# Score matmuls over all 128 rows with a zero-filled second half, and norm factors spread by PE transposes of a broadcast column

## The chip, the core and the metric

The program runs on one core of a Trainium2 chip. The core has five engines that run their own instruction streams and meet through semaphores: PE (TensorE: matrix products, with a separate stream of weight loads, PEld), DVE (VectorE), ACT (ScalarE), POOL (GpSimd) and SP (which issues most DMAs). A matmul multiplies a stationary operand, loaded first, with a moving operand that streams through, and writes to PSUM. The metric is the device time of one execution in microseconds, as the median of several runs. Smaller is better.

## What is computed

Three transformer-like blocks run one after the other on one sequence of 1024 tokens of width 1024, in 32-bit floats. Block 1 mixes differential attention (4 heads, each with two score maps of head size 64) with chunked retention, then a feed-forward layer. Block 2 mixes neighbourhood attention, a convolution, pooling and a gating unit. Block 3 mixes a sliding-window attention (8 query heads of size 64 in 4 groups, a window of 128 tokens), a gated recurrent layer computed in chunks, a cross-attention and a feed-forward layer with a convolution. RMS norms stand between all of them. The parts that the change touches are these:

```python
def rms_norm(x, g, eps=NORM_EPS):
    xf = x.astype(jnp.float32)
    y = xf * lax.rsqrt(jnp.mean(xf * xf, axis=-1, keepdims=True) + eps)
    return (y * g.astype(jnp.float32)).astype(x.dtype)
...
        scores = jnp.einsum('bhmqd,bhmkd->bhmqk', qblk, kt) + bias[None, :, None]
        p = jax.nn.softmax(scores, axis=-1)
        a = p[:, :, 0] - lam * p[:, :, 1]
...
    s = jnp.einsum('bnqhgd,bnkhd->bnhgqk', qb, kw).astype(jnp.float32) * (D ** -0.5)
```

## The kernel before

Features lie on the 128 partitions and tokens on the free axis, in two halves of 512 tokens (`h` is 0 or 1). To keep 32-bit accuracy with the one-pass matmul type, every operand is split into a high and a low part (`split`, L143 on ACT for the high part, L145 on DVE or POOL for the low part), and a product is three matmuls, high by high, high by low and low by high (`mm3`, L178 to L180). `dense` is one output tile of 128 features by 512 tokens: eight such triples, 24 matmuls.

**The scores.** A head has 64 features, so one score map needs 64 rows of the array. The kernel stacks: `qs[m]` holds for map `m` the high part of q on 64 partitions and its low part on the other 64, and `ks[m]` holds the high part of k on both halves (the copies are made by DMA). One matmul over 128 rows (L539, in the window attention L1459) then gives high by high plus low by high. The missing term, q high by k low, is a second matmul into the same PSUM tile over 64 rows alone (L540, L1460), with `kl`, one tile in which map 0 uses partitions 0 to 63 and map 1 partitions 64 to 127. In block 1 `attn_diff` makes these pairs per head, query block, map and stretch of up to 512 keys. DVE then takes the pair's result out of PSUM with bias and row maximum (L544). In block 3 `window` makes them per group, block of 128 queries and map, over 256 keys (128 at the start of the sequence).

**The norm factors.** `rstd` sums squares over features with matmuls against a column of ones (`mean_col`, L204), gets the factor with a power on POOL (`rsqrt_col`, L217, tile `rr`: one column for each 128 tokens, token on the partition), and must then lay it out along the free axis, the same on all partitions (`spread`). `spread` splits the factor into `rh` and `rl` (L225, L227 on DVE), builds two diagonal matrices by multiplying the identity (L231, twice 128x512 on DVE) and adds two matmuls of a matrix of ones with them (L237). DVE reads the result as an operand when it scales (L272, L510, L1268 and others).

**The order of the work.** The kernel is written with generators that interleave streams, and a scheduler places the instructions of each engine by a simulated timeline and a priority; each engine then runs its list strictly in order. Long-lived tiles come from a pool of 37 slots of equal size (`SLOTS`, `slot`); who asks for a slot when none is free waits until all readers of some slot have ended. While a head of `attn_diff` runs, `proj_ret` of the same head and, once slots are free, `proj_diff` of the next supply other matmuls to put between the scores. PSUM tiles of the kind `s` (scores) have three banks in both stages, those of kind `d` (`dense`) two.

Of the kernel before, what the change touches and what calls it, by code (L numbers as in the profile page):

```python
# [18 lines left out]
P = 128  # L19
T = 1024  # L20
# [38 lines left out]
class Env:  # L59
# [160 lines left out]
    def spread(self, r):  # L220

        nc = self.nc
        n = r.shape[-1]
        rh = self.small.tile([P, n], F32R, tag="rh", name="rh")
        nc.vector.tensor_copy(rh, r)  # L225
        rl = self.small.tile([P, n], F32R, tag="rl", name="rl")
        nc.vector.tensor_tensor(rl, r, rh.bitcast(F32), op=ALU.subtract)  # L227
        out = self.pt()[:, : n * P]
        for i, q in enumerate((rh, rl)):
            dg = self.tmp.tile([P, n, P], F32R, tag="diag", bufs=2, name="diag")  # L230
            nc.vector.tensor_tensor(  # L231
                dg,
                self.ident[:, None, :].broadcast_to([P, n, P]),
                q.bitcast(F32)[:, :, None].broadcast_to([P, n, P]),
                op=ALU.mult,
            )
            nc.tensor.matmul(out, lhsT=self.ones_r, rhs=dg.rearrange("p a b -> p (a b)"), start=i == 0, stop=i == 1)  # L237
        return out
# [121 lines left out]
def block1(e, next_gain):  # L360
# [45 lines left out]
    with ExitStack() as c2:  # L406
# [38 lines left out]
        def proj_diff(hd):  # L445

            scale = 0.125 * 2.0 ** (2 * (hd + 1))
            ts = [e.slot("qk", (T,), F32R) for _ in range(5)]
            qs, ks, kl = ts[0:2], ts[2:4], ts[4]
            wq = e.chunk(io["w1_fm"][hd])  # L450
            wk = e.chunk(io["w1_fm"][4 + hd])
            for h in range(2):
                sl = half(h)
                ql = e.tsq(dt=F32R)
                p = normed(e.dense(wq, hs[h]), h)
                for m in range(2):
                    b = slice(64 * m, 64 * m + 64)
                    nc.scalar.activation(qs[m][b, sl], p[b], AF.Copy, scale=scale)
                    nc.vector.scalar_tensor_tensor(ql[b], p[b], scale, qs[m][b, sl].bitcast(F32), op0=ALU.mult, op1=ALU.subtract)
                p = normed(e.dense(wk, hs[h]), h)  # L460
                for m in range(2):
                    b = slice(64 * m, 64 * m + 64)
                    nc.scalar.activation(ks[m][b, sl], p[b], AF.Copy)
                    nc.vector.tensor_tensor(kl[b, sl], p[b], ks[m][b, sl].bitcast(F32), op=ALU.subtract)
                for m in range(2):
                    b = slice(64 * m, 64 * m + 64)
                    o = slice(64 - 64 * m, 128 - 64 * m)
                    nc.sync.dma_start(qs[m][o, sl].bitcast(F32), ql[b].bitcast(F32))
                    nc.sync.dma_start(ks[m][o, sl].bitcast(F32), ks[m][b, sl].bitcast(F32))
# [48 lines left out]
        def attn_diff(hd, ops, v):  # L518
# [3 lines left out]
            for pr in range(4):  # L522
# [6 lines left out]
                for i in range(2):  # L529
# [3 lines left out]
                    for m in range(2):  # L533
                        mx = None
                        pc = []
                        for c, n in cols:
                            s = e.pss()[:, :n]
                            b = slice(64 * m, 64 * m + 64)
                            nc.tensor.matmul(s, lhsT=qs[m][:, blk(qb)], rhs=ks[m][:, c : c + n], start=True, stop=False)  # L539
                            nc.tensor.matmul(s, lhsT=qs[m][b, blk(qb)], rhs=kl[b, c : c + n], start=False, stop=True)  # L540
# [780 lines left out]
def block3(e, acc, hs, rest, out):  # L1321
# [39 lines left out]
    with ExitStack() as c2:  # L1361
# [10 lines left out]
        def stack(w, scale, h, qs, kl=None):  # L1372

            p = e.dense(w, hs[h])
            ql = e.tsq(dt=F32R) if kl is None else kl
            for m in range(2):
# [3 lines left out]
                nc.vector.scalar_tensor_tensor(ql[b], p[b], scale, qs[m][b].bitcast(F32), op0=ALU.mult, op1=ALU.subtract)  # L1380
                nc.sync.dma_start(qs[m][o].bitcast(F32), (ql[b] if kl is None else qs[m][b]).bitcast(F32))
# [36 lines left out]
        kl = e.slot("kl", (T,), F32R)  # L1418
        va = e.slot("va", (8, P))

        def window_kv(h):
            stack(e.chunk(io["w3_fm"][4]), 1.0, h, [k[:, half(h)] for k in ks], kl[:, half(h)])
# [21 lines left out]
        def window(g, h):  # L1444
            qs = ops[g, h][4]
            po = e.po()
            for j4 in range(4):
# [9 lines left out]
                for m in range(2):  # L1457
                    b = slice(64 * m, 64 * m + 64)
                    nc.tensor.matmul(s[m], lhsT=qs[:, m, blk(j4)], rhs=ks[m][:, k0 : k0 + wd], start=True, stop=False)  # L1459
                    nc.tensor.matmul(s[m], lhsT=qs[b, m, blk(j4)], rhs=kl[b, k0 : k0 + wd], start=False, stop=True)  # L1460
# [358 lines left out]
```

## Time and profile before

| | |
|---|---|
| median of 3 runs | 3494.2 us (3491.73 to 3495.17) |
| the profiled execution | 3490.75 us, of which the profile's span is 3489.0 us |
| PE busy | 3329.4 us (95% of the span), 16510 matmuls |
| DVE, ACT, POOL busy | 1922.8 us (55%), 1348.9 us (39%), 894.9 us (26%) |
| mean granted TensorE clock | 0.974 of full speed |

The time of one execution is its span and 1.75 us around it. The profile was taken in an execution that ran 3.45 us under the median of the three runs. A matmul's row gives its start and a modelled duration that overlaps the next matmul; what a matmul costs on PE is read from one start to the next, not from the duration.

### The profile page before, as it was taken

To read this page: it belongs to the slowest core of one execution; us is meant where nothing else is said; L and a number is where in the kernel's file an instruction comes from. 1 tells how busy PE (TensorE), PEld (TensorE's weight loads), DVE (VectorE), ACT (ScalarE), POOL (GpSimd) and SP (SyncE) were. 2 spreads that over 40 slices of the span, in tenths; PEclk is the share of its full clock that TensorE was granted. 3 is DMA by queue.
4 is the path that set the end of the run, shared out by engine and by line. 5 is a ranking of instruction groups with operands and counts; after the bars stand their busy time and mean duration, and the time that the engine had idled before them with its cause. 6 is when DMAs were issued, how large, how long until landed. Compare 5 with 4: busy or idle time off the path is not lost.

```text
span 3489.0 us, 43291 instructions
## 1 busy us (share of the span) xinstructions
PE 3329.4 (95%) x16510; PEld 2737.6 (78%) x16510; DVE 1922.8 (55%) x3463; ACT 1348.9 (39%) x2354; POOL 894.9 (26%) x577
## 2 busy tenths in 40 slices
PE   7999998999999999889999899999899999999997
PEld 6788877888888887677667778878887788888886
DVE  8566566622222238984777575776635771434346
ACT  4444453412211233333544455554443442313132
POOL 2000013401100113521334444435333430202021
PEclk8999999999999999999999999999999999999999
DMA  4112123211111114345644221224423321111114
GB/s 126 46 44 59 49 77 125 94 58 43 46 53 53 43 60 139 115 120 164 204 153 133 74 68 58 82 85 151 151 67 103 133 93 57 47 53 44 53 42 146
DMA packets 122431, 306.23 MB, mean 88 GB/s; under 512 B 17008, under 2 KB 25584, under 8 KB 122224
## 3 DMA queue, kind: packets, MB, share of 16 engines
q1 hardware_dynamic: 122224, 303.47, 27.1%
q8 instruction: 130, 2.13, 0.3%
q14 instruction: 77, 0.63, 0.1%
HBM read 256.23 MB, written 40.37 MB: 85 GB/s over the span
## 4 chain that ended last, share of the span: by engine, by line
PE 38%; DVE 6%; issue 3%; ACT 2%; POOL 1%; DMA 0%; DVEq 0%; POOLq 0%; ACTq 0%
PE ps_d L178 11%; PE ps_d L180 11%; PE ps_d L179 11%; PE ps_s L1548 1%; ACT whi L143 1%; DVE act L145 1%; DVE ssum L263 0%; POOL wlo L145 0%; PE ps_o L1482 0%; PE ps_t L204 0%; DVE hSA L1549 0%; DVE pr L1124 0%; PE ps_s L1460 0%; DVE nq L272 0%; PE ps_d L1559 0%
## 5 line engine op out<-in xcount | busy, mean ns | idle before, releaser
L180 PE MATMUL ps_d<-act,wlo 128*128 128x512 f32 x2272 | 894.2, 394 | 14.5 <-DVE wlo L145 13.2
L178 PE MATMUL ps_d<-act,whi 128*128 128x512 f32 x2272 | 895.6, 395 | 8.0 <-ACT whi L143 4.3
L179 PE MATMUL ps_d<-act,whi 128*128 128x512 f32 x2272 | 895.9, 394 | 3.0 <-DVE act L145 3.0
L143 ACT ACTIVATE whi<-raw 128x1024 fp32r<-128x1024 f32 (+2 forms) x394 | 387.4, 984 | 969.9 <-PE ps_d L179 854.3
L145 POOL TENSOR_TENSOR wlo<-raw,whi 128x1024 fp32r<-128x1024 f32 (+1 forms) x162 | 391.9, 2422 | 740.1 <-ACT whi L143 714.2
L180 PEld LDWEIGHTS ps_d<-act,wlo 128*128 128x128 f32 x2272 | 429.8, 189 | 109.6 <-DVE wlo L145 17.1
L178 PEld LDWEIGHTS ps_d<-act,whi 128*128 128x128 f32 x2272 | 430.0, 189 | 103.3 <-ACT whi L143 9.2
L179 PEld LDWEIGHTS ps_d<-act,whi 128*128 128x128 f32 x2272 | 429.9, 189 | 98.9 <-issue 6.5
L145 DVE TENSOR_TENSOR wlo<-raw,whi 128x1024 fp32r<-128x1024 f32 (+2 forms) x232 | 259.1, 1117 | 276.5 <-ACT whi L143 276.0
L180 PE MATMUL ps_d<-up,wlo 128*128 128x512 f32 x864 | 336.5, 389 | 0.0
L179 PE MATMUL ps_d<-up,whi 128*128 128x512 f32 x864 | 336.2, 389 | 0.0
L178 PE MATMUL ps_d<-up,whi 128*128 128x512 f32 x864 | 335.5, 389 | 0.0
L686 POOL TENSOR_TENSOR nt<-sq 128x512 f32<-128x512 f32 x64 | 83.5, 1305 | 556.0 <-ACT sq L684 555.1
L180 PE MATMUL ps_d<-mix,wlo 128*128 128x512 f32 x512 | 202.6, 396 | 2.9 <-POOL wlo L145 2.9
L178 PE MATMUL ps_d<-mix,whi 128*128 128x512 f32 x512 | 201.1, 399 | 3.3 <-DVE acc L643 2.1
L179 PE MATMUL ps_d<-mix,whi 128*128 128x512 f32 x512 | 203.0, 397 | 0.0
L180 PEld LDWEIGHTS ps_d<-up,wlo 128*128 128x128 f32 x864 | 162.2, 188 | 34.0 <-DVE wlo L145 0.3
L179 PEld LDWEIGHTS ps_d<-up,whi 128*128 128x128 f32 x864 | 162.2, 188 | 33.8
L178 PEld LDWEIGHTS ps_d<-up,whi 128*128 128x128 f32 x864 | 162.2, 188 | 33.7
L693 DVE TENSOR_TENSOR acc<-ps_d,acc 128x512 f32<-128x512 f32 x96 | 66.4, 692 | 203.9 <-PE ps_d L180 203.9
L217 POOL TENSOR_TENSOR rr<-rv,mhalf 128x4 f32<-128x4 f32 (+1 forms) x43 | 45.8, 1065 | 486.3 <-DVE rv L211 274.6
L178 PE MATMUL ps_d<-whi,act 128*128 128x256 f32 x512 | 151.8, 299 | 19.4 <-ACT act L388 12.6
(404 smaller groups left out, 5528.5 us busy)
## 6 DMA issues: line engine op xcount, KB each, us to landing
raw<-in_w_up SPq DMA_DIRECT2D x94, 512.0 KB, 3.3
raw<-in_w_fm SPq DMA_DIRECT2D x84, 512.0 KB, 3.6
raw<-in_w_out SPq DMA_DIRECT2D x42, 512.0 KB, 3.3
raw<-in_w_down SPq DMA_DIRECT2D x64, 320.0 KB, 3.0
xd<-acc SPq DMA_DIRECT2D x64, 256.0 KB, 2.4
acc<-xd SPq DMA_DIRECT2D x64, 256.0 KB, 5.5
raw<-in_w_down SPq DMA_DIRECT2D x32, 384.0 KB, 3.2
raw<-in_w_tm SPq DMA_DIRECT2D x22, 512.0 KB, 3.3
```

What stands on the lines that cost most here:

```text
L143: nc.scalar.activation(hi, src, AF.Copy)
L145: e.tensor_tensor(lo, src, hi.bitcast(F32), op=ALU.subtract)
L178: nc.tensor.matmul(out, lhsT=wh, rhs=xh, start=start, stop=False)
L179: nc.tensor.matmul(out, lhsT=wh, rhs=xl, start=False, stop=False)
L180: nc.tensor.matmul(out, lhsT=wl, rhs=xh, start=False, stop=stop)
L217: self.nc.gpsimd.tensor_tensor(r, v, self.mhalf.broadcast_to([P, n]), op=ALU.pow)
L686: nc.gpsimd.tensor_tensor(u, r, r, op=ALU.mult)
L693: nc.vector.tensor_tensor(acc[f][:, h], p, acc[f][:, h], op=ALU.add)
L1548: nc.tensor.matmul(s[:, blk(j, 64)], lhsT=x[:, blk(j)], rhs=xv[:, nb * j : nb * j + nb, 1], start=True, stop=True)
```

## The change

The change has two parts.

*Scores.* `kl` becomes two tiles, one for each map, both 128 partitions high. The 64 partitions that the map does not use are set to zero once by POOL (two memsets of 64x1024 for each head in `proj_diff`, two in the window attention). The second score matmul then runs over all 128 rows, with the same stationary operand as the first. Each of the two attentions holds one slot more: six instead of five for a head's q and k, and one more for the whole window stage.

*Norm factors.* `spread` no longer splits the factor or builds diagonals. For each of the (usually four) columns it transposes that column, read 128 times with a step of zero, on PE against the identity. The 128x128 result has the factor of token t in column t on all partitions.

```diff
     def spread(self, r):
-        rh = self.small.tile([P, n], F32R, tag="rh", name="rh")
-        nc.vector.tensor_copy(rh, r)
-        rl = self.small.tile([P, n], F32R, tag="rl", name="rl")
-        nc.vector.tensor_tensor(rl, r, rh.bitcast(F32), op=ALU.subtract)
         out = self.pt()[:, : n * P]
-        for i, q in enumerate((rh, rl)):
-            dg = self.tmp.tile([P, n, P], F32R, tag="diag", bufs=2, name="diag")
-            nc.vector.tensor_tensor(dg, self.ident[:, None, :]..., q..., op=ALU.mult)
-            nc.tensor.matmul(out, lhsT=self.ones_r, rhs=dg..., start=i == 0, stop=i == 1)
+        for i in range(n):
+            nc.tensor.transpose(out[:, blk(i)], r[:, i : i + 1].broadcast_to([P, P]), self.ident)
         return out
...
         def proj_diff(hd):
-            ts = [e.slot("qk", (T,), F32R) for _ in range(5)]
-            qs, ks, kl = ts[0:2], ts[2:4], ts[4]
+            ts = [e.slot("qk", (T,), F32R) for _ in range(6)]
+            qs, ks, kl = ts[0:2], ts[2:4], ts[4:6]
+            for m in range(2):
+                nc.gpsimd.memset(kl[m][64 - 64 * m : 128 - 64 * m].bitcast(F32), 0.0)
...
-                            nc.tensor.matmul(s, lhsT=qs[m][b, blk(qb)], rhs=kl[b, c : c + n], start=False, stop=True)
+                            nc.tensor.matmul(s, lhsT=qs[m][:, blk(qb)], rhs=kl[m][:, c : c + n], start=False, stop=True)
...
-        kl = e.slot("kl", (T,), F32R)
+        kl = [e.slot(f"kl{m}", (T,), F32R) for m in range(2)]
+        for m in range(2):
+            nc.gpsimd.memset(kl[m][64 - 64 * m : 128 - 64 * m].bitcast(F32), 0.0)
...
-                    nc.tensor.matmul(s[m], lhsT=qs[b, m, blk(j4)], rhs=kl[b, k0 : k0 + wd], start=False, stop=True)
+                    nc.tensor.matmul(s[m], lhsT=qs[:, m, blk(j4)], rhs=kl[m][:, k0 : k0 + wd], start=False, stop=True)
```

The scheduler places everything anew, so instructions shift by a few places all over the program. Three places show what moves. The first is PE in the first head of `attn_diff`, where single score pairs stand between projection matmuls (`ps_s` is a score tile, `ps_d` a projection, `ps_t` a transpose). Before:

```order
L178 MATMUL ps_d<-act,whi 128x512
L539 MATMUL ps_s<-qk 128x512
L540 MATMUL ps_s<-qk 128x512
L179 MATMUL ps_d<-act,whi 128x512
L180 MATMUL ps_d<-act,wlo 128x512
L178 MATMUL ps_d<-act,whi 128x512
```

After, the same place:

```order
L178 MATMUL ps_d<-act,whi 128x512
L558 MATMUL ps_t<-ident,prob 128x128
L529 MATMUL ps_s<-qk 128x512
L530 MATMUL ps_s<-qk 128x512
L179 MATMUL ps_d<-act,whi 128x512
L180 MATMUL ps_d<-act,wlo 128x512
```

A transpose has moved in front of the pair, and the pair itself stands as it stood; the lines 529 and 530 are the old 539 and 540. The second place is DVE at the end of the program, from the last mean to the last scaling. Before:

```order
L207 TENSOR_SCALAR rv<-ps_t 128x4
L225 CAST rh<-rr 128x4
L227 TENSOR_TENSOR rl<-rr,rh 128x4
L231 TENSOR_TENSOR diag<-ident,rh 128x512
L231 TENSOR_TENSOR diag<-ident,rl 128x512
L1268 SCALAR_TENSOR_TENSOR acc<-acc,g_ffn_post_norm_14656,ps_t 128x512 x8
```

After, DVE has two rows there, and PE's list ends with the four mean columns and four transposes of the factor:

```order
L207 TENSOR_SCALAR rv<-ps_t 128x4
L1258 SCALAR_TENSOR_TENSOR acc<-acc,g_ffn_post_norm_14512,ps_t 128x512 x8
```

```order
L204 MATMUL ps_t<-ones_r,ssum 128x1 x4
L226 MATMUL ps_t<-ident,rr 128x128 x4
```

The four DVE instructions between mean and scaling are gone. The third place is POOL at the change from head 0 to head 1 of block 1 (`rr` is a norm factor, `nt` a gated output of the retention). Before:

```order
L217 TENSOR_TENSOR rr<-rv,mhalf 128x4 x3
L512 TENSOR_TENSOR nt<-nt,gate 128x512
L217 TENSOR_TENSOR rr<-rv,mhalf 128x4
L512 TENSOR_TENSOR nt<-nt,gate 128x512
L217 TENSOR_TENSOR rr<-rv,mhalf 128x4 x3
```

After, the same place:

```order
L217 TENSOR_TENSOR rr<-rv,mhalf 128x4
L440 MEMSET qk 64x1024 x2
L217 TENSOR_TENSOR rr<-rv,mhalf 128x4 x2
L503 TENSOR_TENSOR nt<-nt,gate 128x512
L217 TENSOR_TENSOR rr<-rv,mhalf 128x4
L503 TENSOR_TENSOR nt<-nt,gate 128x512
```

The two memsets of the next head stand between the two factors of the differential attention, so a factor of the same head waits behind them.

## Rows read from the trace of the kernel before

**Rows 1.** The profile page: span, and each engine's busy time (share, xinstructions).
```profile
span 3489.0 us, 43291 instructions
...
PE 3329.4 (95%) x16510; PEld 2737.6 (78%) x16510; DVE 1922.8 (55%) x3463; ACT 1348.9 (39%) x2354; POOL 894.9 (26%) x577
```

**Rows 2.** Busy time by stretch: PE, PEld, DVE, ACT, POOL, granted clock, DMA share, GB/s.
```profile
110.00:480.00 370.00, 369.34 (x2041) 302.65 (x2040) 216.96 (x550) 164.56 (x361) 20.92 (x18) 1.00 0.17 51
1950.00:2350.00 400.00, 377.56 (x2200) 313.21 (x2200) 270.50 (x634) 225.47 (x443) 180.15 (x154) 0.94 0.22 71
```

**Rows 3.** PE's groups, shapes apart: rows*columns, xcount, busy, mean ns, idle before.
```profile
L540 PE MATMUL ps_s<-qk 64*128 64x512 f32 x64 | 32.4, 506 | 0.0
...
L1460 PE MATMUL ps_s<-kl,swq 64*128 64x256 f32 x56 | 22.5, 402 | 0.0
...
L540 PE MATMUL ps_s<-qk 64*128 64x256 f32 x32 | 12.8, 400 | 0.0
...
L1460 PE MATMUL ps_s<-kl,swq 64*128 64x128 f32 x8 | 2.6, 323 | 0.0
```

**Rows 4.** Timeline of PE in block 1's attention: start, duration, instruction.
```profile
88.85 0.39 PE L178 MATMUL ps_d<-act,whi 128*128 128x512 f32 x1
89.08 0.40 PE L539 MATMUL ps_s<-qk 128*128 128x512 f32 x1
89.40 0.50 PE L540 MATMUL ps_s<-qk 64*128 64x512 f32 x1
89.83 0.50 PE L179 MATMUL ps_d<-act,whi 128*128 128x512 f32 x1
90.17 0.40 PE L180 MATMUL ps_d<-act,wlo 128*128 128x512 f32 x1
```

**Rows 5.** Timeline of the weight loads at the same place.
```profile
89.40 0.18 PEld L540 LDWEIGHTS ps_s<-qk 64*128 64x128 f32 x1 [0.36 <-issue]
...
90.17 0.19 PEld L178 LDWEIGHTS ps_d<-act,whi 128*128 128x128 f32 x1
```

**Rows 6.** Timeline of PE in block 3's window attention, a pair over 256 keys.
```profile
2172.24 0.28 PE L1459 MATMUL ps_s<-k,swq 128*128 128x256 f32 x1
2172.44 0.38 PE L1460 MATMUL ps_s<-kl,swq 64*128 64x256 f32 x1
2172.75 0.50 PE L179 MATMUL ps_d<-act,whi 128*128 128x512 f32 x1
2173.09 0.39 PE L180 MATMUL ps_d<-act,wlo 128*128 128x512 f32 x1
```

**Rows 7.** Timeline of PE, two full-height matmuls of 256 columns in a row.
```profile
2188.52 0.28 PE L179 MATMUL ps_d<-wlo,act 128*128 128x256 f32 x1
2188.64 0.28 PE L180 MATMUL ps_d<-whi,act 128*128 128x256 f32 x1
```

**Rows 8.** Timeline of PE around three transposes.
```profile
91.33 0.49 PE L568 MATMUL ps_t<-ident,prob 128*128 128x128 f32 x3
...
91.89 0.39 PE L180 MATMUL ps_d<-act,wlo 128*128 128x512 f32 x1
```

**Rows 9.** Timeline at the program's last norm, all engines.
```profile
3472.84 1.02 POOL L217 TENSOR_TENSOR rr<-rv,mhalf 128x4 f32<-128x4 f32 x1 [9.59 <-DVE rv L207]
...
3474.92 1.40 PE L237 MATMUL ps_t<-diag,ones_r 128*128 128x512 f32 x2 [2.35 <-DVE diag L231]
...
3476.35 4.04 DVE L1268 SCALAR_TENSOR_TENSOR acc<-acc,g_ffn_post_norm,ps_t 128x512 f32<-128x512 f32 x6 [0.89 <-PE ps_t L237]
```

**Rows 10.** What PE waited for: us in total, times, longest.
```profile
PE ps_t L237 <- DVE diag L231: 14.1, 7, 3.0
...
PE ps_s L539 <- ACT act L143: 4.3, 1, 4.3
```

**Rows 11.** DVE's group of the first of the two diagonals.
```profile
L231 DVE TENSOR_TENSOR diag<-ident,rh 128x512 fp32r<-128x512 f32 x46 | 31.5, 685 | 7.1 <-PE ps_t L237 7.1
```

**Rows 12.** POOL's group of the memset that is nearest in size.
```profile
L875 POOL MEMSET cb<- 128x1024 f32 x2 | 1.9, 952 | 0.0
```

More of the change, by code (lines that the diff above doesn't have):

```diff
@@ L223, in spread @@
         n = r.shape[-1]
-        rh = self.small.tile([P, n], F32R, tag="rh", name="rh")
-        nc.vector.tensor_copy(rh, r)
-        rl = self.small.tile([P, n], F32R, tag="rl", name="rl")
-        nc.vector.tensor_tensor(rl, r, rh.bitcast(F32), op=ALU.subtract)
         out = self.pt()[:, : n * P]
-        for i, q in enumerate((rh, rl)):
-            dg = self.tmp.tile([P, n, P], F32R, tag="diag", bufs=2, name="diag")
[L231 to L237, printed above, removed]
+        for i in range(n):
+            nc.tensor.transpose(out[:, blk(i)], r[:, i : i + 1].broadcast_to([P, P]), self.ident)
         return out
@@ L463, in proj_diff @@
                     nc.scalar.activation(ks[m][b, sl], p[b], AF.Copy)
-                    nc.vector.tensor_tensor(kl[b, sl], p[b], ks[m][b, sl].bitcast(F32), op=ALU.subtract)
+                    nc.vector.tensor_tensor(kl[m][b, sl], p[b], ks[m][b, sl].bitcast(F32), op=ALU.subtract)
                 for m in range(2):
@@ L1374, in stack @@
             p = e.dense(w, hs[h])
-            ql = e.tsq(dt=F32R) if kl is None else kl
+            if kl is None:
+                ql = e.tsq(dt=F32R)
             for m in range(2):
@@ L1379, in stack @@
                 nc.scalar.activation(qs[m][b], p[b], AF.Copy, scale=scale)
-                nc.vector.scalar_tensor_tensor(ql[b], p[b], scale, qs[m][b].bitcast(F32), op0=ALU.mult, op1=ALU.subtract)
-                nc.sync.dma_start(qs[m][o].bitcast(F32), (ql[b] if kl is None else qs[m][b]).bitcast(F32))
+                lo = ql[b] if kl is None else kl[m][b]
+                nc.vector.scalar_tensor_tensor(lo, p[b], scale, qs[m][b].bitcast(F32), op0=ALU.mult, op1=ALU.subtract)
+                nc.sync.dma_start(qs[m][o].bitcast(F32), (lo if kl is None else qs[m][b]).bitcast(F32))
         v = {}
@@ L1417, in block3 @@
         ks = [e.slot(f"k{m}", (T,), F32R) for m in range(2)]
-        kl = e.slot("kl", (T,), F32R)
+        kl = [e.slot(f"kl{m}", (T,), F32R) for m in range(2)]
+        for m in range(2):
+            nc.gpsimd.memset(kl[m][64 - 64 * m : 128 - 64 * m].bitcast(F32), 0.0)
         va = e.slot("va", (8, P))
         def window_kv(h):
-            stack(e.chunk(io["w3_fm"][4]), 1.0, h, [k[:, half(h)] for k in ks], kl[:, half(h)])
+            stack(e.chunk(io["w3_fm"][4]), 1.0, h, [k[:, half(h)] for k in ks], [k[:, half(h)] for k in kl])
             p = e.dense(e.chunk(io["w3_fm"][5]), hs[h])
@@ L1457, in window @@
                 for m in range(2):
-                    b = slice(64 * m, 64 * m + 64)
                     nc.tensor.matmul(s[m], lhsT=qs[:, m, blk(j4)], rhs=ks[m][:, k0 : k0 + wd], start=True, stop=False)
-                    nc.tensor.matmul(s[m], lhsT=qs[b, m, blk(j4)], rhs=kl[b, k0 : k0 + wd], start=False, stop=True)
+                    nc.tensor.matmul(s[m], lhsT=qs[:, m, blk(j4)], rhs=kl[m][:, k0 : k0 + wd], start=False, stop=True)
                     nc.vector.tensor_tensor_reduce(pr[:, m, :wd], s[m], swm[:, w0:], scale=-1.0,
```

1 line of the change is left out of this document (removed).

## The prediction

> **What bounds the kernel now.** I read the page's busy times first: PE has 95% of the span, the next engine, DVE, 55% [rows 1]. Then the table by stretch, for the two stages in which the score matmuls lie. In block 1's attention PE is busy for 369.34 of 370 us; in the window stage of block 3 for 377.56 of 400 us, with a mean granted clock of 0.94 [rows 2]. So in the first stage whatever PE saves is saved in full until another engine gets in the way, and in the second most of it. Then PE's timeline, start to start, because a busy PE may still be a slow one. What is to be seen there: between projection matmuls 512 columns cost 0.23 us (88.85 to 89.08), but around a score pair the starts are 0.32, 0.43 and 0.34 us apart [rows 4]. The weight load of the 64-row matmul starts only together with its matmul, 0.36 us after the previous load ended, with no engine waited for; the load of a projection matmul (90.17) starts one matmul ahead (90.41 is its turn) [rows 5]. So a change of height from 128 to 64 rows and back stops the overlap, and the 64-row matmul saves nothing for that: it streams as many columns.
>
> **Scores, what goes.** From the start of L539 to that of the second projection matmul behind the pair are 90.17 - 89.08 = 1.09 us [rows 4]. Three full-height matmuls of 512 columns would take 3 x 0.23 = 0.69. The excess is 0.40 us for one 64-row matmul. In the window stage the same stretch is 2173.09 - 2172.24 = 0.85 us [rows 6], against 0.12 + 0.12 + 0.23 = 0.47, since a full-height matmul of 256 columns costs 0.12 [rows 7]: an excess of 0.38. There are 64 such matmuls of 512 columns and 32 of 256 in block 1, 56 of 256 and 8 of 128 in block 3 [rows 3]. For the 8 I take 0.30, an estimate below the other two. Block 1: 64 x 0.40 + 32 x 0.38 = 37.8 us; block 3: 56 x 0.38 + 8 x 0.30 = 23.7 us; together 61.5 us of PE's time.
>
> How much reaches the end? In block 1 nothing but PE's own work is in the way now, but DVE is busy for 217 of 370 us [rows 2], 65% of what would be left, and it must empty a pair before the third one after it can reuse its bank. With pairs at 0.46 us instead of 0.86, runs of pairs without a projection between them will meet DVE. I count 0.85 of 37.8, 32 us, and between 0.6 and 1 for the range. In the window stage PE already waits for 22 of 400 us, in chains through DVE, ACT and POOL which the change leaves; I count 0.7 of 23.7, 17 us, between 0.4 and 1. Forecast 49 us, range 32 to 61.5.
>
> **Scores, what comes.** Ten memsets of 64x1024 on POOL; the nearest row is 128x1024 at 0.95 us [rows 12], with as many elements on a partition, so about 9.5 us in all. POOL is busy for 21 of 370 us in block 1 [rows 2], and what is queued behind a head's pair there is one factor `rr` whose scaling is needed a projection later: nothing. In front of block 3 the pair stands ahead of low parts of the next inputs, for which PE may wait: 0 to 1.9 us, I take 1. The memset needs a slot, and block 1 has none to spare: 16 inputs, 4 v, 5 q and k, 4 for probabilities, 3 for their transposes and 5 for the next `proj_ret` are 37. With six for q and k the gate, the last of these five, waits until the head's scores have been read. Its matmuls can still fill the two `ps_d` banks; the next projection then waits for the gate to leave PSUM, about 0.6 us a head, 2 us in all. The bound is the first rival below. DMAs, and the queue that issues them, are as before.
>
> **Norm factors.** On PE two matmuls of 0.23 us become four transposes. Three transposes and a projection matmul take 91.89 - 91.33 = 0.56 us [rows 8], so a transpose costs 0.11 and four 0.44: no difference. No row shows a load that reads one column 128 times. Its lower bound is this price, since the columns that stream are the same; the upper bound is a load that hides behind nothing, 0.19 us [rows 5] for each of about 47 x 4, 36 us. I take the price of the transpose, the nearest row.
>
> On DVE two diagonals of 0.69 us [rows 11] and two small operations go from each of 47 spreads, some 1.7 us each, 80 us in all. Hidden behind a busy PE this is worth nothing; DVE is not the bound. It counts where PE stood waiting: 14.1 us at 7 spreads [rows 10]. At the last norm the factor is there at 3472.84 + 1.02 = 3473.86 and DVE scales from 3476.35, 2.49 us later [rows 9]. Four transposes right behind the factor would leave about 1.0, an estimate of twice 0.44 at a low clock and the way to DVE: 1.5 us saved. For 7 places that is 10 us. In the first 75 us PE waited 4.3 us for DVE and ACT to finish normed inputs [rows 10], and two spreads stand in DVE's queue there: up to 3.4 us, I count 2. With a discount for waits that another engine takes over I forecast 11 us, range 4 to 18.
>
> **The sum.** 49 + 11 - 1 - 2 = 57 us off the profiled execution: 3490.75 - 57 = 3433.75. That execution lies 3.45 us under the median of the runs, so 3437 us. The ends: 32 + 4 - 4 = 32 us, and 61.5 + 18 = 79.5 us, so 3462 and 3415.
>
> **Rivals.** *The slot ends it on the other side: slower.* If the 38th slot is what decides, the stretch in which PE has nothing to put between the scores grows. The gate's 48 matmuls are 11 us a head (48 x 0.23); if they were no cover any more in 4 heads, 44 us, and if in block 3 one tile of 24 matmuls (5.5 us) came too late in each of 8 units, 44 more. 3437 + 88 = 3525. It decides from about 57 us on, 4.8 us of new idle time in each of the 12 places. Against it: in the new order PE keeps projection matmuls between the pairs. Chance 0.04.
>
> *The gain meets the other engines.* PE empties its list sooner, and the chain from score through DVE and ACT to the transposes sets the pace in both stages. Then only some 40% of 61.5, 25 us, arrive: 3490.75 - 25 - 11 + 3 + 3.45 = 3461. For it: DVE's 65%, the 0.94 clock and the idle 22 us of the window stage. Chance 0.13.
>
> *The broadcast load is slow.* 36 us come back: 3437 + 36 = 3473. Chance 0.06.
>
> *The weight loads stay exposed.* If consecutive loads of full height did not overlap the running matmul, a pair would cost 2 x (0.23 + 0.19) = 0.84 us where it now costs 1.09 - 0.23 = 0.86, and 160 pairs would give 3 us: 3490.75 - 3 - 11 + 3 + 3.45 = 3483. The row of 90.17 speaks against it: the load runs under a matmul of the same height [rows 5]. The Trainium skill's page "TensorE: Matmul & The Clock Gate" (Part 3, packing small matmuls) has the rule by which it would come so: loads overlap matmuls in flight only where their row groups differ, and a matmul of few rows costs what one of 128 rows costs. By that rule this change would gain next to nothing on the scores; the trace agrees with the second half (same columns, same streaming) and not with the first. Chance 0.03.
>
> *The clock gains too.* In the window stage 0.06 of 400 us, 24 us, are lost to stretches granted 1.2 instead of 2.4 GHz [rows 2]. If fewer stops leave none of them, 3437 - 24 = 3413. Nothing in the rows promises it. Chance 0.06.
>
> **How the numbers follow.** The forecast (3437) has 0.68. Its own ends, 3415 and 3462, contain the second rival's time and reach the last but two; the range 3408 to 3463 takes in the clock and leaves out the slow load, the exposed loads and the slot, 0.13, and some of the rest. A measurement of this kernel tells about 0.2%, 7 us, from no change. Faster by more than that, under 3487: all but the slot and a part of the exposed loads, 0.93. Same 0.03, slower 0.04.
>
> **What would show it.** Right: rows of the second score matmul with 128 rows, a pair and its two successors spaced 0.23 us at 512 columns, loads one matmul ahead; PE's waits for the diagonal gone, and DVE scaling about 1 us after the last factor. DVE's busy time falls by 80 us. Wrong on the cover: new waits of PE for score banks or for the gate in block 1, and a span of 110 to 480 us that shrinks by less than 30. Wrong on the load: transposes of `rr` more than 0.11 us apart.

## The result, and the profile after

The changed kernel takes 3442.4 us (median of 4 runs, 3440.0 to 3446.7) against 3493.8 us for the kernel before in the same comparison: a ratio of 0.985, 95% interval 0.984 to 0.987. That is 51 us less; 3437 was forecast. In the comparisons of the experiments below, the kernel before has lower medians, 3488.4 to 3491.0 us, so the 51 us may be 3 to 5 too many. The profiled execution of after has a span of 3441.4 us against 3489.0 [rows 1], 47.6 us less.

The page of after: span, and busy time of each engine (share, xinstructions).

```profile
span 3441.4 us, 43369 instructions
...
PE 3270.4 (95%) x16602; PEld 2736.9 (80%) x16602; DVE 1850.7 (54%) x3275; ACT 1344.7 (39%) x2354; POOL 909.3 (26%) x587
```

PE is busy for 59 us less and DVE for 72 us less; PE still has 95% of the span. Lines have moved by the edit: L540 of before is L530, L1460 is L1453, L237 is L226, L1268 is L1258.

The stretches of the prediction in the kernel after (us of the stretch; busy PE, PEld, DVE, ACT, POOL; granted clock, DMA share, GB/s), then the two stages by their own ends, from the first to the last score matmul of block 1 (70.8 to 472.0) and of the window attention (1907.1 to 2310.0).

```profile
110.00:480.00 370.00, 366.61 (x2206) 326.09 (x2205) 214.52 (x540) 179.92 (x394) 30.84 (x28) 1.00 0.19 59
1950.00:2350.00 400.00, 372.65 (x2282) 319.18 (x2281) 248.86 (x558) 223.36 (x430) 175.29 (x138) 0.95 0.23 75
70.80:472.00 401.20, 395.90 (x2319) 349.11 (x2320) 239.95 (x613) 192.58 (x431) 34.03 (x30) 0.98 0.19 57
1907.10:2310.00 402.90, 364.63 (x2223) 312.88 (x2222) 264.21 (x611) 231.14 (x452) 182.18 (x154) 0.93 0.21 70
```

The same two stages in the kernel before:

```profile
72.70:510.30 437.60, 435.46 (x2302) 349.62 (x2302) 263.80 (x666) 199.82 (x439) 30.83 (x25) 0.98 0.18 54
1946.40:2350.00 403.60, 379.22 (x2208) 314.20 (x2207) 273.14 (x643) 227.39 (x449) 181.56 (x154) 0.94 0.22 70
```

The fixed stretches [rows 2] mislead here, since the work has moved up within them; the stages by their own ends come closer to the same work. In the window stage PE's list differs only by the spreads (transposes for matmuls with diagonals); in block 1's stage it also has 9 projection matmuls of 512 columns less, some 2.1 us, which now lie outside it. They say where the time went. Block 1's stage is 36.4 us shorter. In the window stage PE is busy for 14.6 us less, and the stage is 0.7 us shorter: what PE saved there became idle time (403.6 - 379.2 = 24.4 us before, 402.9 - 364.6 = 38.3 after). TensorE's granted clock has two levels in these traces, full and half (2.4 and 1.2 GHz); PE spent 58.0 us of this stage at the lower one, 51.2 before, which also took a part. The other 10 us lie in the start (1.9 us), between the two stages (0.9), behind the window stage (4.4), in the last feed-forward (1.9) and the tail (1.3).

PE's timeline in block 1 after: start, duration, instruction.

```profile
88.07 0.28 PE L178 MATMUL ps_o<-probT,vh 128*128 128x256 f32 x1
88.19 0.39 PE L529 MATMUL ps_s<-qk 128*128 128x512 f32 x1
88.41 0.39 PE L530 MATMUL ps_s<-qk 128*128 128x512 f32 x1
88.64 0.40 PE L529 MATMUL ps_s<-qk 128*128 128x512 f32 x1
88.88 0.39 PE L530 MATMUL ps_s<-qk 128*128 128x512 f32 x1
89.11 0.28 PE L529 MATMUL ps_s<-qk 128*128 128x256 f32 x1
```

The weight loads at the same place:

```profile
88.41 0.19 PEld L529 LDWEIGHTS ps_s<-qk 128*128 128x128 f32 x1
88.64 0.19 PEld L530 LDWEIGHTS ps_s<-qk 128*128 128x128 f32 x1
88.88 0.19 PEld L529 LDWEIGHTS ps_s<-qk 128*128 128x128 f32 x1
```

Starts of 512 columns are 0.22 to 0.24 us apart, in a pair and between pairs, where they were 0.32, 0.43 and 0.34 [rows 4]. Each load runs under the matmul in front (the load for the matmul of 88.64 starts at 88.41, with the matmul ahead of it), where the load of 64 rows started only with its own matmul [rows 5]. The Trainium skill's page "TensorE: Matmul & The Clock Gate" (Part 3) says in its list of what overlaps that loads overlap matmuls in flight only where their row groups differ; this trace contradicts that line, since here they are the same 128 rows. (The same part also lets loads run ahead that go to a background weight buffer; the trace does not contradict that.) Its page "TensorEngine Tiling (Array Packing)" (Key Properties) says that changing the tiling mode drains the engine; if a change of height counts as one, rows 4 and these rows agree.

One of after's spreads and the last norm. First PE around the spread, in block 1:

```profile
191.24 0.28 PE L180 MATMUL ps_d<-whi,act 128*128 128x256 f32 x1
191.36 0.60 PE L226 MATMUL ps_t<-ident,rr 128*128 128x128 f32 x4
191.71 0.37 PE L178 MATMUL ps_d<-whi,act 128*128 128x256 f32 x1
191.92 0.29 PE L179 MATMUL ps_d<-wlo,act 128*128 128x256 f32 x1
```

Four transposes and a projection matmul of 256 columns take 191.92 - 191.36 = 0.56 us; less 0.12 for the matmul [rows 7] that is 0.11 a transpose, as for an ordinary one [rows 8]. A load that reads one column 128 times costs nothing extra. The last norm, all engines:

```profile
3426.56 1.02 POOL L217 TENSOR_TENSOR rr<-rv,mhalf 128x4 f32<-128x4 f32 x1 [11.87 <-DVE rv L207]
...
3427.63 1.12 PE L226 MATMUL ps_t<-ident,rr 128*128 128x128 f32 x4 [1.35 <-POOL rr L217]
3428.78 3.38 DVE L1258 SCALAR_TENSOR_TENSOR acc<-acc,g_ffn_post_norm,ps_t 128x512 f32<-128x512 f32 x5 [2.31 <-PE ps_t L226]
```

DVE scales 3428.78 - 3427.58 = 1.20 us behind the factor, where it was 2.49 [rows 9]. What PE waited for in the whole span (us, times, longest), the groups that answer to [rows 10]:

```profile
PE ps_s L529 <- ACT act L143: 4.9, 1, 4.9
...
PE ps_t L226 <- DVE rr L233: 3.2, 1, 3.2
...
PE ps_t L226 <- POOL rr L217: 2.3, 3, 1.4
```

The 14.1 us of waits for a diagonal have become 5.5 us of waits for the factor itself. The wait of 4.3 us for `act` at the first scores has not gone: 4.9. PE's idle time in the whole span has not fallen: 3489.0 - 3329.4 = 159.6 us before, 3441.4 - 3270.4 = 171.0 after.

### The profile page after: what moved, and what is told of

Same layout as the page of the kernel before. It is cut to its first block, busy times and chain, and to the rows that moved or that the text cites. A ratio compares the mean times of both kernels' runs of the same rounds, so it can differ in the third digit from the quotient of the medians.

```text
span 3441.4 us, 43369 instructions
## 1 busy us (share of the span) xinstructions
PE 3270.4 (95%) x16602; PEld 2736.9 (80%) x16602; DVE 1850.7 (54%) x3275; ACT 1344.7 (39%) x2354; POOL 909.3 (26%) x587
## 4 chain that ended last, share of the span: by engine, by line
PE 38%; DVE 7%; issue 3%; ACT 2%; POOL 1%; DMA 0%; DVEq 0%; ACTq 0%; POOLq 0%; SPq 0%
PE ps_d L178 11%; PE ps_d L179 11%; PE ps_d L180 11%; ACT whi L143 1%; DVE acc L1258 1%; PE ps_s L1541 0%; PE ps_t L204 0%; DVE hE L1527 0%; DVE hSA L1542 0%; PE ps_d L1552 0%; DVE act L145 0%; DVE acc L1259 0%; DVE pr L1114 0%; POOL wlo L145 0%; DVE ssum L252 0%
## 5 line engine op out<-in xcount | busy, mean ns | idle before, releaser
L180 PE MATMUL ps_d<-act,wlo 128*128 128x512 f32 x2272 | 893.1, 394 | 15.4 <-DVE wlo L145 15.4
L180 PEld LDWEIGHTS ps_d<-up,wlo 128*128 128x128 f32 x864 | 162.3, 188 | 33.5
L179 PEld LDWEIGHTS ps_d<-up,whi 128*128 128x128 f32 x864 | 162.3, 188 | 33.5
L178 PEld LDWEIGHTS ps_d<-up,whi 128*128 128x128 f32 x864 | 162.3, 188 | 33.5
```

What stands on the lines that cost most here:

```text
L178: nc.tensor.matmul(out, lhsT=wh, rhs=xh, start=start, stop=False)
L179: nc.tensor.matmul(out, lhsT=wh, rhs=xl, start=False, stop=False)
L180: nc.tensor.matmul(out, lhsT=wl, rhs=xh, start=False, stop=stop)
```

## The experiments

Each ratio is against the kernel before, in the same comparison. Each kernel's comparison had a median of before between 3488.4 and 3491.0 us.

**One part alone: block 1's scores.** The kernel before with only this edit (and its zero rows):

```
-  nc.tensor.matmul(s, lhsT=qs[m][b, blk(qb)], rhs=kl[b, c : c + n], start=False, stop=True)
+  nc.tensor.matmul(s, lhsT=qs[m][:, blk(qb)], rhs=kl[m][:, c : c + n], start=False, stop=True)
```

> The kernel before with the new score pairs in block 1 alone (two zero-padded kl tiles, 128-row second matmul); spread and the window attention are the old ones. If a change of height costs PE what was read from the starts, 37.8 us of PE's time go in the stretch from the first to the last score matmul of block 1, and that stretch falls from 437.7 us by 33 to 38, as in the changed kernel (401.3); the time is about 3494 - 36 = 3458. If instead the lighter DVE queue (spread) was needed for the score gain to arrive, the stretch falls by less than 28 and PE shows new waits for DVE's row maxima.

Measured: 3457.2 us, ratio 0.992 (0.990 to 0.993), some 29 us. The stage of block 1 takes 404.8 us for 437.6, 32.8 less, just under the range that was expected. Its busy times, and the longest new wait of PE in it:

```profile
72.00:476.80 404.80, 396.11 (x2302) 348.00 (x2303) 259.89 (x665) 197.57 (x438) 36.30 (x30) 0.99 0.19 58
PE ps_o L178 <- ACT o L577: 4.9, 3, 1.7
```

The stage holds the same matmuls as before, in another order. PE is busy for 39.4 us less, some 4 of them by the clock (6.8 us at the lower level for 14.8, of which half is lost), and idle for 8.7 us instead of 2.1: it waits for ACT to take the output of the attention out of PSUM, and once for a score bank (1.2 us). Of the 37.8 us that the prediction worked out for PE, 32.8 are 0.87, but without the clock 0.76. A pair of runs with the same order is better placed to tell; it comes with the run without zero rows.

**One part alone: the spread.** Only the new `spread`:

```
-  ...   (two diagonals on DVE, two matmuls of 512 columns)
+  for i in range(n):
+      nc.tensor.transpose(out[:, blk(i)], r[:, i : i + 1].broadcast_to([P, P]), self.ident)
```

> The kernel before with the new spread alone; all score pairs are old. If spread counts only where PE stood waiting for a diagonal and at the start, the time falls by 8 to 14 us, to about 3483, spread over the start, the two stages before and behind the window attention and the tail. If its worth was less than forecast (the places only pass the wait on), by 0 to 5 us. In the stretch from the first to the last window score matmul (403.7 us before) nothing should change by more than 3 us.

Measured: 3476.6 us, ratio 0.997 (0.995 to 0.998), 12 us. But the 12 is a sum of both signs. Its page has a span of 3475.3 us and these busy times:

```profile
PE 3313.5 (95%) x16602; PEld 2734.7 (79%) x16602; DVE 1847.7 (53%) x3275; ACT 1349.0 (39%) x2356; POOL 896.5 (26%) x577
```

Busy time of its stages of block 1 and of the window attention:

```profile
72.00:503.20 431.20, 429.14 (x2318) 348.09 (x2318) 242.48 (x613) 195.72 (x432) 28.35 (x24) 0.99 0.17 53
1933.30:2343.20 409.90, 379.44 (x2224) 314.86 (x2222) 263.14 (x611) 230.72 (x452) 183.04 (x154) 0.94 0.21 69
```

Block 1 gains 6.4 us, at a clock of 0.99 for 0.98; 11 projection matmuls of 512 columns, some 2.5 us, have moved out of the stage. The window stage, in which nothing was expected to change by more than 3 us, loses 6.3: PE is busy as long as before (379.44 for 379.22) and idle for 30.5 us instead of 24.4, though DVE has 10 us less to do. The spread changes the order of PE's instructions there (86% of its rows stand in the same sequence as before), and I could not separate that from the spread itself. The rest of the gain lies at the start (0.7), between the stages (6.0), behind the window stage (3.4), in the last feed-forward (1.9) and the tail (1.6).

The page says what kind of gain this is. PE is idle for 3475.3 - 3313.5 = 161.8 us in the whole span, against 159.6 before: the waits for diagonals are gone, but as much waiting has come elsewhere. What fell is PE's busy time, by 15.9 us, and the time at the lower clock level fell from 179.3 to 152.0 us, of which half is 13.7. That is not this one execution alone: over the six executions the mean granted clock is 0.9773, over 21 of before 0.9748, some 9 us less lost. Among 58 executions of before, one that loses 1 us more to the lower level is on average 0.6 us longer; so I put 5 to 9 of the 12 us down to the clock, an estimate. Why the clock is granted more in this kernel is not shown.

**One part alone: the window scores.** L1460 and its zero rows as in the change, all else as before.

> The kernel before with the new score pairs in the window attention alone; spread and block 1 are old. The changed kernel gained 0.7 us in this stretch where 23.7 us of PE's time went. If the chain through DVE, ACT and POOL sets the pace there, the same here: the stretch stays at 400 to 404 us, and PE's waits in it rise from 24 us by 10 to 20. If it was the new order of this one build or the new spread that ate the gain, the stretch falls by 10 to 20 us.

Measured: 3486.4 us, ratio 0.999 (0.998 to 1.000): nothing that is certain. The window stage:

```profile
1946.50:2348.50 402.00, 363.78 (x2209) 312.24 (x2208) 271.32 (x643) 227.47 (x449) 183.06 (x154) 0.92 0.22 70
```

PE is busy for 15.4 us less and idle for 13.8 more (38.2 for 24.4), and it spends 61.4 us at the lower clock level for 51.2. This looks as if the window part alone made the 0.7 us of the changed kernel; the run without the window part, below, shows that those are another sum.

**Is it the height, or the number of matmuls?** The kernel before, with block 1's 64-row matmul of 512 columns split into two of 256:

```
-  nc.tensor.matmul(s, lhsT=qs[m][b, blk(qb)], rhs=kl[b, c : c + n], start=False, stop=True)
+  for d in range(0, n, 256):
+      nc.tensor.matmul(s[:, d : d + 256], lhsT=qs[m][b, blk(qb)], rhs=kl[b, c + d : c + d + 256], start=False, stop=d + 256 >= n)
```

> The kernel before with every 64-row matmul of 512 columns in block 1 cut into two of 256 columns that follow each other. Columns and changes of height stay the same, the number of 64-row matmuls rises by 64. If the cost lies in the change of height, the time from the first full-height matmul of a pair to the second projection matmul behind it stays at 1.09 to 1.13 us, and block 1's score stretch stays at 437.7 us within 4. If each 64-row matmul stops the overlap by itself, 0.2 to 0.4 us come for each of the 64: 13 to 26 us more in that stretch.

Measured: 3493.8 us, ratio 1.001 (1.000 to 1.002); the stage 441.4 us for 437.6. PE's timeline there:

```profile
82.56 0.51 PE L539 MATMUL ps_s<-qk 128*128 128x512 f32 x1
83.00 0.50 PE L541 MATMUL ps_s<-qk 64*128 64x256 f32 x2
83.43 0.50 PE L539 MATMUL ps_s<-qk 128*128 128x512 f32 x1
```

Their weight loads:

```profile
83.00 0.29 PEld L541 LDWEIGHTS ps_s<-qk 64*128 64x128 f32 x2 [0.25 <-issue]
```

Two matmuls of 64 rows in a row take 83.43 - 83.00 = 0.43 us, which is 2 x 0.12 for the columns and 0.19 once. Their two loads, of 0.18 us each [rows 5], are done in 0.29 us: the second starts under the first matmul, so a load of 64 rows does overlap where the height stays. The stage is 3.8 us longer with 64 more matmuls, at most 0.06 each (11 projection matmuls, some 2.5 us, have also moved into it, and the clock gave some 2 us back); if each paid the excess of 0.40 it would be 26 us. The excess belongs to the change of height, about 0.19 us each way, and not to a matmul of 64 rows.

**The slots and memsets without the use.** The kernel before, which holds one slot more through the window stage and clears it:

```
   kl = e.slot("kl", (T,), F32R)
+  held = e.slot("held", (T,))
+  nc.gpsimd.memset(held[64:128], 0.0)
+  nc.gpsimd.memset(held[0:64], 0.0)
...
+  nc.vector.tensor_copy(mxl, held[:, 0:4])
```

> The kernel before with one slot taken at the place where kl is taken in block 3 (filled with zeros by POOL, read once by DVE behind the window stage) and nothing else changed: the cost of the slot and its memsets alone. If the slot is what ate the gain in the window stage, the stretch of the window scores rises from 403.7 us by 8 to 20. If not, it stays within 4 us, and the time is 3488 to 3495.

Measured: 3490.2 us, ratio 1.0005 (0.9995 to 1.0014); the window stage 402.5 us for 403.7, at 44.4 us of lower clock for 51.2. PE's order in the stage is that of before. Held in that order, the slot does not decide.

**The changed kernel without the window part** (block 1 and spread).

> The changed kernel with the old score pairs in the window attention: block 1 and spread are changed. If the window part is worth what it is worth alone (2 us), the time is 3443 to 3448. If spread lengthens the window stage on its own (409.8 us with spread alone, 403.7 before) and the cheaper pairs take that back, the stretch is 408 to 412 us and the time 3448 to 3454.

Measured: 3446.7 us, ratio 0.988 (0.986 to 0.989): the time as in the first reading, the stage as in the second. Its window stage is longer than that of before, as with the spread alone, whose order of instructions it has in this stage:

```profile
1897.00:2309.20 412.20, 381.28 (x2222) 316.41 (x2221) 264.29 (x611) 230.19 (x452) 182.50 (x154) 0.93 0.21 69
```

So in the changed kernel the window stage hides two things of opposite sign: the kernels with the new spread take 6 to 9 us more (the upper end with 58.0 us at the lower clock for 51.2), and the window scores give 9 us back (402.9 for 412.2, at the same 58.0 us). In medians the part is worth 4 us, in ratios 8.

**Does PE's time count in the window stage at all?** The changed kernel without the window attention's second score matmul.

> The changed kernel without the second score matmul of the window attention (the term q high by k low is left out there, so the scores are slightly less exact). That takes another 64 matmuls, about 8 us of PE's time, out of the stretch of the window scores (402.9 us in the changed kernel) and no work from any other engine. If the chain through DVE, ACT and POOL sets the pace, the stretch stays at 399 to 406 us and PE's waits in it grow from 38 us by 5 to 10. If PE's time still counts there, it falls by 6 to 10 us.

Measured: 3436.8 us, ratio 0.985 (0.983 to 0.986). The window stage:

```profile
1908.00:2303.20 395.20, 356.66 (x2161) 302.95 (x2159) 260.21 (x611) 229.08 (x451) 182.13 (x154) 0.93 0.22 71
```

64 matmuls of 0.12 us are 7.7 us; the stage is 7.7 us shorter, and PE is idle for 38.5 us as with them. A chain through the other engines that sets the pace throughout would have kept the stage at 402. That theory fell in its plain form. (PE's order is another here, too: 89% of its rows stand in the sequence of the changed kernel, so the two numbers agree more closely than one pair of traces can promise.)

**The k-low tiles outside the slots.** The changed kernel with `kl` of the window stage in a pool of its own, so that it takes no slot.

> The changed kernel with the two zero-padded kl tiles of the window attention in a pool of their own, so that this stage has one slot more than before the change instead of one less. If the second slot of kl held projections back and so ate the gain, the stretch of the window scores (402.9 us) falls by 8 to 20 us, to 3425 to 3435 in all. If the chain sets the pace, it stays within 4 us, about 3442.

Measured: 3437.7 us, ratio 0.985 (0.983 to 0.986); the window stage 405.5 us, 2.6 longer, with 68.3 us at the lower clock for 58.0, which is some 5 of them. So it is at most 2 to 3 us shorter by itself, within the 4 of the second reading: the slots do not hold the window stage.

**The old order, and full height.** This run was to tell the chain from the new order. The window attention's second matmul goes over all 128 rows of the tiles that it already had:

```
-  nc.tensor.matmul(s[m], lhsT=qs[b, m, blk(j4)], rhs=kl[b, k0 : k0 + wd], start=False, stop=True)
+  nc.tensor.matmul(s[m], lhsT=qs[:, m, blk(j4)], rhs=kl[:, k0 : k0 + wd], start=False, stop=True)
```

On PE, DVE, ACT and POOL all instructions stand in the order of before, row for row, in the whole program.

> The kernel before, with the window attention's second score matmul over all 128 rows of the tiles that it has already: lhsT is the whole of qs for map m and rhs the whole of the one kl tile. The other 64 rows then add the product of map m's q low with the other map's k low, an extra term of the output that is left in. No memset, no further slot, no further tile; the order of the instructions on all engines is the same as that of the kernel before, row for row, so a new order can't be what happens to the time. All theories: TensorE's busy time in the window stretch falls by 13 to 24 us (the run with the window part alone and the changed kernel showed 15 in a stretch of that length). Theory 1, the chain through VectorE, ScalarE and GpSimd sets the pace of the window stretch: TensorE's idle time there rises by 9 to 18 us against 24.4, the stretch stays within 398 to 405 us of 403.7, and the kernel within 6 us of before (3488 to 3494). Theory 2, the scheduler's new order took the gain away (it differs in 2.6% of TensorE's rows in the run with the window part alone): with the old order the stretch falls to 382 to 392 us and the kernel to 3470 to 3482.

Measured: 3483.5 us, ratio 0.9985 (0.9976 to 0.9994). The stage falls by 7.2 us, between both theories: PE's timeline at the place of [rows 6], and the stage.

```profile
2167.38 0.28 PE L1459 MATMUL ps_s<-k,swq 128*128 128x256 f32 x1
2167.50 0.28 PE L1460 MATMUL ps_s<-kl,swq 128*128 128x256 f32 x1
2167.62 0.40 PE L179 MATMUL ps_d<-act,whi 128*128 128x512 f32 x1
2167.85 0.40 PE L180 MATMUL ps_d<-act,wlo 128*128 128x512 f32 x1
```

```profile
1946.30:2342.80 396.50, 364.68 (x2209) 313.24 (x2208) 272.05 (x643) 227.25 (x449) 183.39 (x154) 0.92 0.22 71
```

At that place the three steps take 0.47 us for 0.85, as forecast. Since the order is the same, PE's 2207 intervals from start to start in the stage can be subtracted one by one from those of before, and each difference divided into idle time, time at the lower clock outside it (half of it is lost) and the rest:

| intervals | count | difference, us | idle | clock | rest |
|---|---|---|---|---|---|
| first score matmul | 64 | -6.6 | 0.0 | -0.6 | -6.0 |
| second score matmul | 64 | -8.0 | +2.8 | -0.6 | -10.2 |
| the one behind it | 57 | -4.1 | 0.0 | +0.1 | -4.2 |
| all others | 2022 | +11.4 | +4.6 | +5.3 | +1.5 |
| sum | 2207 | -7.3 | +7.4 | +4.2 | -18.9 |

PE saves 20.4 us at the pairs (0.32 for each of 64). Waits take 7.4 back, the lower clock 4.2, the other intervals 1.5. The same subtraction of the run without the window part from the one without zero rows (below), whose PE orders in this stage are also the same, gives -19.8 at the pairs, +7.8 of idle time, -3.1 of clock, +3.2 at the others, together -12.0. How much of this is chance shows in the run with the held slot, whose order is also that of before: +1.9 of idle time, -3.6 of clock, +0.5 of the rest. So about 7 to 8 us of idle time come with the faster pairs, in the same order; the clock falls one way or the other. Where the waits are, for PE in this stage (us, times, longest), first before:

```profile
PE ps_d L1559 <- DVE hSA L1549: 6.3, 6, 1.9
PE ps_t L1477 <- DVE pr L1472: 4.3, 3, 3.6
...
PE ps_s L1548 <- POOL hE L1535: 1.4, 2, 0.9
```

and with the old order and full height:

```profile
PE ps_d L1559 <- DVE hSA L1549: 7.6, 6, 2.6
PE ps_t L1477 <- DVE pr L1472: 6.0, 4, 3.9
PE ps_s L1548 <- POOL hE L1535: 3.2, 4, 1.1
```

They are the waits of before, each somewhat longer: for `hSA` and `hE` of the recurrent core and for the probabilities. With the window part alone, in the scheduler's new order, the idle time rises by 13.8 instead of 7.4, and the stage gains 1.7 instead of 7.2. The time at the lower clock is the same in both (61.4 us). The new order is the likely place of the other 5 to 6 us; only this pair of runs shows it.

**No zero rows at all.** All three parts, with the trick of the last run in both stages: no memsets, no further slots.

> All three parts of the change, but without zero rows: in block 1 and in the window attention the second score matmul goes over all 128 rows of the tiles of the kernel before (one k-low tile for both maps, so that the other 64 rows add q low by k low of the other map, an extra term that is left in). No memsets of 1024 columns, two slots fewer than the changed kernel needs at its fullest. Theory slots and memsets cost nothing (the run that only held them showed 3490 against 3494): 3438 to 3447, the same as the changed kernel's 3442.4. Rival, the slots do cost in the changed kernel, by the 0.8 us wait of the gate and the later loads: 3430 to 3438. By theory 1 of the run before (chain sets the pace in the window) the window stretch stays at 400 to 413 us; by theory 2 (new order) it is 385 to 395, since here the order of the window is that of the kernel with spread and block 1 alone.

Measured: 3433.6 us, ratio 0.984 (0.983 to 0.986); the window stage 400.4 us, block 1's 395.3. That is below the range of the first theory and in that of the rival, but its interval overlaps that of the changed kernel. The window stage is at the lower end of theory 1.

Its stage of block 1 also gives the clean measure of the scores there: the run with the spread alone has the same instructions in the same order on PE, DVE, ACT and POOL.

```profile
70.70:466.00 395.30, 391.29 (x2318) 345.43 (x2319) 239.88 (x613) 194.44 (x432) 28.27 (x24) 1.00 0.19 58
```

Interval by interval, as above: -35.2 us at the 96 pairs (0.37 each), +2.0 of idle time, -2.6 of clock, -0.3 at the others, together -36.1. Without the clock that is 33.5 us of the 37.8 worked out for PE, 0.89.

**One slot more,** 38 for 37, for the changed kernel and for the one without zero rows.

> The changed kernel with one slot more in the pool of slots (38 for 37), which gives back the slot that the second k-low tile takes. A candidate to beat both. Theory slots cost nothing: 3438 to 3446, the stretches of the changed kernel within 3 us each but for the places where half clock falls. Rival, the slot costs: 3430 to 3437, with the 0.8 us wait of ScalarE's gate in block 1 gone and the block-1 stretch 1 to 3 us shorter.

> The kernel of the run without zero rows (3433.6, ratio 0.9844) with 38 slots for 37, as a candidate that beats both. Theory, slots do not set the pace anywhere: 3430 to 3440, ratio 0.983 to 0.986, no stretch of the kernel more than 3 us from the run without zero rows except where half clock falls otherwise. Rival, the one slot more lets loads and gates go earlier by as much as the slot that the 38-slot run of the changed kernel had back: 3424 to 3430. The output has the same extra term of q low by k low of the other map.

Measured: 3436.0 us, ratio 0.985 (0.983 to 0.986), and 3440.8 us, 0.986 (0.984 to 0.987). The first is in the range of the rival, and so are its signs: the wait for the gate is gone, and block 1's stage is shorter.

```profile
71.80:467.10 395.30, 391.21 (x2317) 345.46 (x2318) 239.99 (x613) 194.35 (x432) 34.03 (x30) 1.00 0.19 58
```

With 37 slots this stage stands in one order in four traces, the changed kernel (401.2 us, with 12.9 us at the lower clock) and the three variants of its window stage (398.6 each, with 3.2 to 3.4). With 38 slots it takes 395.3, with 3.4 us at the lower clock, in the order of the spread alone. So the slot is worth some 3 us in block 1: the wait for the gate (0.8 us) and those for ACT's emptying of `o` (2.5 us, twice) are gone. The run without zero rows has no memsets in this stage and the same order on PE, DVE and ACT, and takes the same 395.3: the memsets cost nothing there.

The second has less in its way than the kernel without zero rows and is no faster; its block 1 takes 404.1 us, in another order, with 25 projection matmuls more inside the stage. None of these variants is shown to beat the changed kernel: their ratios lie between 0.984 and 0.986, and all intervals overlap its own.

## Why the prediction was right, and where it was not

*PE is the bound, and the excess is a change of height.* Right. The rows of after show it, the run with two halves shows that the cost is the change and not the matmul, and block 1's term came as counted: 33.5 us without the clock, in the same order, for 32. The factor 0.85 stood for DVE; of the 4 us that are missing, 2 are idle time and the rest a saving of 0.37 instead of 0.39 us a pair.

*The window term was mis-sized.* The prediction counted 0.7 of 23.7 us, 17. The window part measured 2 us alone (interval -1 to 6), 4 in medians and 9 in the stage on top of the other two parts, and 5 (2 to 8) with the order held. Two steps failed. The smaller one: 0.38 us was read from one pair [rows 6] and taken for all; over the 64 pairs it is 0.32. The first interval gives back 0.09 us wherever the pair stands. But behind 19 of the pairs comes no projection but a transpose or another small matmul (L1477, L1482, L1548), and there, with the old order, the second interval gives 0.10 to 0.17 us instead of 0.19 and the one behind it 0.00 to 0.04 instead of 0.10. The larger one: the factor 0.7 took the 22 us of idle time as they were. They grew by 7 to 8 us: PE comes sooner to the chains of the core and of the window attention, and the lists above show the same waits, longer. And the time at the lower clock, which the prediction held constant, moved what is lost by -3 to +4 us. The second rival had this mechanism right, but at too high a price and for both stages: in the window stage it takes somewhat over a third of the gain (7.4 of 20.4 us), in block 1 2.0 of 35.2.

*The spread: right in size by luck.* 11 us were forecast and 12 measured. The tail came as said (1.3 us for 1.5), the transposes cost what an ordinary one costs, and the waits at spreads fell from 14.1 to 5.5 us. But the step from there to the time failed: the prediction took a wait that goes for time that is saved, and with the spread alone PE's idle time in the whole span did not fall (161.8 us for 159.6). The window stage alone has 6 us more of it. The start gave 1.9 us for 2 in the changed kernel, but the wait for `act` that was to go is still there. The 12 us are for a large part less time at the lower clock, which the prediction did not have. In block 1 that is half of the 6.4 us (8.6 us for 14.8, of which half counts), and most of the other half are the 11 matmuls that moved out of the stage. DVE's busy time fell by 72 us, where 80 were counted.

*The costs.* The memsets cost 0.95 us each as forecast:

```profile
L440 POOL MEMSET qk<- 64x1024 f32 x8 | 7.6, 949 | 56.7 <-PE ps_s L530 37.9 <-ACT whi L143 18.5
```

POOL stood for 37.9 us until scores had been read, which is the slot that the prediction spoke of, and nobody waited for it. The gate's wait is there once, 0.8 us, where 2 us were counted in four heads; with the waits for `o` that the 37-slot order brings, the slot costs some 3 us in block 1:

```profile
PE ps_d L178 <- ACT gate L477: 0.8, 1, 0.8
```

The rival of the slot fell: nothing of the size of its 88 us is there. A held slot costs nothing in the old order, tiles outside the slots do not shorten the window stage, and a 38th slot gains some 3 us in block 1 and nothing certain in the whole time.

*The sum* came within 6 us of the median, by errors of both signs, so its closeness is luck in part. Of the 57 us off the profiled execution 47.6 came. Block 1's scores are as counted; the window's are 8 us too high by its stage and 12 with the order held; the waits that went at the spreads came back as others, 6 us of them in the window stage; and against that stand the clock and places between the stages that were not counted. The 3.45 us from the profiled execution to the median of three runs hide some of the miss: in the later comparisons the medians of before are 2.3 us under to 0.3 above that execution.

## What to carry to other kernels

Look at matmuls that use part of the rows: if the neighbours use all of them, it is the change of height that costs, and either zero rows or a group of equal heights pays it off. A saving on the busiest engine counts stage by stage: where that engine already waits a little, some of the saving turns into longer waits at the same places, so read the existing waits as a chain that does not move. A wait that goes in one place can come back in another: look at the engine's idle time in the whole span, and at the time at each clock level, before a gain is put down to it. To separate a saving from a new order, make a variant with the same tiles and the same order, and subtract the two traces instruction by instruction.

## What the runs showed of the hardware

A change between 128 and 64 rows costs about 0.19 us each way at 512 and at 256 columns, and the load of the weights then does not run under the matmul ahead; two 64-row matmuls in a row pay it once for the pair, and the second one's load runs under the first. A transpose whose input is one column read 128 times takes 0.11 us, as an ordinary one does. The time at the lower of the two clock levels differs by up to 10 us in a stage whose instructions stand in the same order: in the window stage 51.2 us before and 61.4 with full height, and in block 1's stage, which is the same code in the same order, 12.9 us in the changed kernel and 3.2 to 3.4 in the three variants of its window stage.
